# The end of a block unit in the first embedding stage, queued on ScalarE behind the copy between its PSUM banks

## The chip, the core and the metric

The kernel runs on one core of one Trainium2 chip. The metric is the device time of one execution in microseconds (us), as a median over runs. Engine names are those of the profile: PE is TensorE's matmul and PEld its weight load, DVE is VectorE, ACT is ScalarE, POOL is GpSimd, SP is SyncE, which issues most of the DMAs.

## The reference

Two layers of a decoder trunk on 512 tokens with 1024 features, all in float32. Each layer is a mixer (layer 0: windowed attention beside a short convolution; layer 1: chunked gated linear attention), a gated MLP with a causal convolution, and a per-layer embedding; each adds to x.

```python
for i in range(DEPTH):
    h = _rms_norm(x, mix_norm[i])
    x = x + (attn_conv_mixer(h) if i % 2 == 0 else gla_mixer(h))
    x = x + _conv_ffn(_rms_norm(x, ffn_norm[i]), ...)
    x = x + _per_layer_embedding(x, p[i], ple_norm[i], ple_w_gate[i], ple_w_proj[i])

def _per_layer_embedding(x, p_i, norm, w_gate, w_proj):
    gate = jax.nn.sigmoid(_rms_norm(x, norm) @ w_gate)      # 1024 x 1024
    return gate * (p_i @ w_proj)                            # 256 x 1024
```

The change lies in the embedding of layer 0, the function `ple0`. What it leaves behind, x after the embedding, is the input of layer 1's mixer: the gated linear attention, whose first step is again an RMS norm and a projection.

## The kernel before

**Data.** x stays in SBUF as `xT`, eight tiles of 128 features by 512 tokens. A float32 product is made of three matmuls of rounded halves: each operand is split into a rounded high part h and the remainder l, and h·h, h·l and l·h are summed (`mm3`, lines 162 to 164; lines 879 to 881 inside a block product). Such a split costs one ScalarE instruction (the rounding, L109 or L112) and one VectorE instruction (the remainder, L110 or L113). Weights are split the same way when they have been loaded: L142 and L143 in `cut`, L826 and L827 in `cut_blocks`. The high parts go into tiles called `wh`, of which there are three buffers; the low parts go into `wl`.

**The norm.** The scale 1/rms of a token is applied after the product, as the tile `R`. So a stage that changes x ends each feature tile m by writing the rounded product of x and the next norm's gain (`b`, by L112 and L113), by squaring x on ScalarE (L1369 for m = 0, L1372 after it) and by adding the squares into `acc` on VectorE (L1373). When all eight are there, TensorE transposes `acc` (L329), and VectorE sums it (L331).

**The embedding stage of layer 0.** The gate's 1024 output features are made in four units of two tiles (256 features). Units 0 and 1 are plain products (`plain`). Units 2 and 3 are block units: a 2 by 2 block product in seven products instead of eight (`seven`), whose parts run in this order on TensorE, with these copies between PSUM banks on ScalarE:

```python
        product(X[:, left], plain, 1, tokens(1, 0))
        product(Y[:, left], t2, 0, s2)
        self.copied = nc.scalar.copy(X[:, right], Y[:, left])
        yield
        last = self.cut_blocks(od)
        product(X[:, right], t13, 1, s3)
        self.turned_over = nc.scalar.copy(Y[:, right], X[:, right])
        yield
        product(Y[:, left], last, 1, s4)
        product(X[:, right], last, 0, tokens(1, 1))
        yield X, Y, more
```

The first copy shown is L900, the second, `turned_over`, is L904. The product behind L904 writes the bank that L904 writes too, so it waits for it. `seven` is a generator: the loop of `ple0` places other matmuls at its `yield`s.

**The loop.** `ple0` goes over u = 1, 2, 3. Turn u makes the gate's unit u (plain for u = 1, a block unit for u = 2 and 3) and ends the unit before it: it applies the sigmoid to the gate of tiles 2u - 2 and 2u - 1 (L1358), projects p for these two tiles (`proj`, two steps of three matmuls each), and calls `finish` for each. The last unit is ended after the loop. In turn u = 2 or 3 the two projections stand between the parts of the block product; the first tile's projection and the first step of the second come ahead of the product whose end releases L904, and the second's second step, three matmuls, stands between that product and the product that waits for L904. In u = 2 the loop also cuts unit 3's weights, in a context `tc.issue_after(self.turned_over.ins)`.

`finish(m, s, pj)` does six to seven things for one tile: on VectorE the gate times the projection (L1363), x plus that (L1364), the remainder of the rounding (L113) and the sum of squares (L1373); on ScalarE the rounding (L112) and the squares (L1372, or L1369). It issues no DMA and no matmul.

**What sets the order.** Inside this stage TensorE's order is the order of the program (`tc.manual_schedule(engines={ET.PE})`). The other engines' queues are ordered by the framework's planner: it goes through the program in a simulated time and gives each engine the instruction that is ready, the one traced earlier first. `tc.issue_after(ins)` adds, to each instruction that the block traces on the engine of `ins`, an edge of order: it is put behind `ins` on that engine's queue, without a wait for its end. Other engines get no such edge. In layer 1's mixer the planner orders TensorE too.

Of the kernel before, what the change touches and what calls it, by code (L numbers as in the profile page):

```python
# [56 lines left out]
class Kernel:  # L57
# [1235 lines left out]
    def ple0(self, fp):  # L1293

        nc, a, tc = self.nc, self.a, self.tc
        xg, forms = self.xg, []
        wg = a["ple_w_gate"][0].rearrange("(k p) n -> p k n", p=P)
        wp = a["ple_w_proj"][0].rearrange("(k p) n -> p k n", p=P)  # L1300
        units = ND // 2

        def loaded(u):
            raw = self.raw(ND, 2 * P)
            nc.sync.dma_start(raw, wg[:, :, 2 * P * u : 2 * P * (u + 1)])
            return raw

        def sums(j):
            rows = [self.fp.tile([P, S], F32, tag=tag, name=self.nm("sum")) for tag in ("b0", "b0", "b1", "b1")]
            for u in range(2):  # L1310
                m = 2 * j + u
                nc.scalar.activation(rows[u], self.xT[m], AF.Copy, scale=self.g_ple[0][:, m : m + 1])
            forms.append(self.block_sums(rows))

        def square():
            return fp.tile([P, S], F32, tag="z", name=self.nm("z"), bufs=3)

        def sevens(u):

            raw = loaded(u)  # L1320
            ev, od = self.by_parity(raw)
            first = self.first_forms(ev, od, raw)
            yield
            t13 = self.cut_blocks(ev)
            yield self.seven(od, (first, t13, self.more_forms(ev, od)), xg, forms, square)

        def plain(w, c):
            pg = self.ps()
            for k in range(ND):
                self.mm3(pg, w(k, c * P, (c + 1) * P), xg[k], start=k == 0, stop=k == ND - 1)  # L1330
            return pg

        def projection():
            raw = self.raw(2, D)
            nc.sync.dma_start(raw, wp)
            h, l = (self.four(fp).rearrange("p (k c) n -> p k (c n)", k=2) for _ in range(2))
            for k in range(2):
                nc.scalar.activation(h[:, k], raw[:, k], AF.Copy)
                nc.vector.tensor_tensor(l[:, k], raw[:, k], h[:, k].bitcast(F32), ALU.subtract)
            return h, l  # L1340

        def proj(m):

            pj = self.ps()
            c = slice(m * P, (m + 1) * P)
            for k in range(2):
                self.mm3(pj, (wph[:, k, c], wpl[:, k, c]), pT[k], start=k == 0, stop=k == 1)
                yield pj

        def sigmoid(pg, more=None):  # L1350
            s = self.half()
            if more is None:
                nc.vector.tensor_tensor(s, pg, R, ALU.mult)
            else:
                h2 = lambda x: x.rearrange("p (u t) -> p u t", u=2)
                nc.vector.tensor_tensor(h2(s), h2(pg), more.unsqueeze(1).to_broadcast([P, 2, S // 2]), ALU.add)
                nc.vector.tensor_tensor(s, s, R, ALU.mult)
            nc.scalar.activation(s, s, AF.Sigmoid)  # L1358
            return s

        def finish(m, s, pj):
            x = self.xT[m]
            nc.vector.tensor_tensor(s, s, pj, ALU.mult)  # L1363
            nc.vector.tensor_tensor(x, x, s, ALU.add)  # L1364
            hl = self.pair(self.fp, "b0", "b1")
            self.split(hl, x, self.g_mix[1][:, m : m + 1])
            self.xg.append(hl)
            if m == 0:
                nc.scalar.activation(self.acc, x, AF.Square)  # L1369
            else:  # L1370
                sq = square()
                nc.scalar.activation(sq, x, AF.Square)  # L1372
                nc.vector.tensor_tensor(self.acc, self.acc, sq, ALU.add)  # L1373

        src = a["p"][0, 0].rearrange("(t p) e -> p t e", p=P)
        pin = [fp.tile([P, NT, P], F32, tag="z", name=self.nm("pin"), bufs=3) for _ in range(2)]
        for e in range(2):
            nc.sync.dma_start(pin[e], src[:, :, e * P : (e + 1) * P])
        w = self.cut(loaded(0), "b")
        for j in range(ND // 2):  # L1380
            sums(j)
        with tc.manual_schedule(engines={ET.PE}):
            gates = [plain(w, 0)]
            self.end_norm()
            w1 = self.cut(loaded(1), "b")
            gates.append(plain(w, 1))
            R = self.spread()
            pT = self.load_p(0, fp, pin)
            wph, wpl = projection()
            self.begin_norm(("b0", "b1"))  # L1390
            def sigmoids():
                return [sigmoid(*(g if isinstance(g, tuple) else (g,))) for g in gates]

            ready = sevens(2)
            next(ready)
            steps = next(ready)
            for u in range(1, units):
                m = 2 * u - 2
                gates = sigmoids()
                pjs = [proj(m + c) for c in range(2)]  # L1400
                if u == 1:
                    new = []
                    for c in range(2):
                        new.append(plain(w1, c))
                        next(pjs[c])
                        pjs[c] = next(pjs[c])
                else:
                    more = u + 1 < units
                    if more:
                        ready = sevens(u + 1)  # L1410
                        next(ready)
                    next(steps)
                    next(pjs[0])
                    next(steps)
                    pjs[0] = next(pjs[0])
                    next(pjs[1])
                    next(steps)
                    if more:
                        with tc.issue_after(self.turned_over.ins):
                            after = next(ready)  # L1420
                    pjs[1] = next(pjs[1])
                    X, Y, V = next(steps)
                    new = [X, (Y, V)]
                    if more:
                        steps = after
                for c in range(2):
                    finish(m + c, gates[c], pjs[c])
                gates = new
            gates = sigmoids()
            for c in range(2):  # L1430
                pj = proj(ND - 2 + c)
                next(pj)
                finish(ND - 2 + c, gates[c], next(pj))
            self.end_norm()
# [648 lines left out]
```

## Time and profile before

| what | us |
|---|---|
| median of 3 runs (lowest to highest) | 1204.29 (1204.18 to 1205.54) |
| the profiled execution | 1203.8 |
| its span, first to last instruction | 1202.0 |
| PE busy in it | 1194.0 |
| DVE busy | 989.3 |
| ACT busy | 681.1 |
| granted TensorE clock | 1.00 of full speed |

The profile is of one execution. Its times count from the span's start; the embedding stage of layer 0 lies between about 530 and 586 us. A row of a timeline shows the start, the duration, the engine, the line of the kernel, the operation and its tiles, and in brackets the idle time of the engine before it with what ended that. Matmuls are pipelined: the distance between two starts is shorter than the duration of one, and the distance is what counts.

### The profile page before, as it was taken

The numbers are of one execution on the slowest core, as the hardware profiler recorded it, in microseconds if no ns is written. First come the engines' busy times: TensorE is split into PE (matmuls) and PEld (weight loads), VectorE is DVE, ScalarE is ACT, GpSimd is POOL, SyncE is SP. The second block draws the span as 40 slices with busy tenths as digits, with TensorE's granted clock in tenths as the row PEclk, the third lists the DMA queues.
The fourth block names the chain that finished last, engine by engine and source line by source line (L and its number), as shares of the span: only waits on it lengthen the run. The fifth ranks groups of instructions, "written<-read, shape, count | busy, mean of one in ns | idle before, by whom it ended". The sixth has DMA issues, their size and how long they took to land.

```text
span 1202.0 us, 17888 instructions
## 1 busy us (share of the span) xinstructions
PE 1194.0 (99%) x7085; PEld 1037.6 (86%) x7085; DVE 989.3 (82%) x1563; ACT 681.1 (57%) x1109; POOL 43.7 (4%) x64
## 2 busy tenths in 40 slices
PE   9999999999999999999999999999999999999998
PEld 8877788999899889888988988889999999888887
DVE  6786587899999996789769876677999999978595
ACT  7466465656555744566563555565555656645374
POOL 2600000000000000000100000000000000000000
PEclk9999999999999999999999999999999999999999
DMA  7221322323233342232422222313242423322501
GB/s 222 90 88 39 97 79 70 129 83 119 92 104 107 107 139 97 97 106 63 140 66 69 71 71 70 106 54 122 71 140 71 139 72 128 127 88 97 210 1 70
DMA packets 110839, 117.61 MB, mean 98 GB/s; under 512 B 2808, under 2 KB 105778, under 8 KB 110756
## 3 DMA queue, kind: packets, MB, share of 16 engines
q1 hardware_dynamic: 109920, 115.88, 29.7%
q8 instruction: 55, 0.90, 0.3%
q0 software_dynamic: 560, 0.42, 0.3%
q10 hardware_dynamic: 276, 0.18, 0.1%
q14 instruction: 28, 0.23, 0.1%
HBM read 114.37 MB, written 2.10 MB: 97 GB/s over the span
## 4 chain that ended last, share of the span: by engine, by line
PE 89%; DVE 6%; ACT 2%; issue 1%; POOL 1%; DMA 0%; SPq 0%; DVEq 0%; ACTq 0%; POOLq 0%
PE ps L162 11%; PE ps L163 11%; PE ps L164 11%; PE pa L163 7%; PE pa L162 7%; PE pa L164 7%; PE ps L879 6%; PE ps L881 6%; PE ps L880 6%; PE pa L879 2%; PE pa L881 2%; PE pa L880 2%; DVE wl L143 1%; PE ps L1484 1%; PE ps L1483 1%
## 5 line engine op out<-in xcount | busy, mean ns | idle before, releaser
L142 ACT ACTIVATE wh<-raw 128x1024 fp32r<-128x1024 f32 (+4 forms) x146 | 145.8, 999 | 124.5 <-PE ps L163 78.8
L143 DVE TENSOR_TENSOR wl<-raw,wh 128x1024 fp32r<-128x1024 f32 (+4 forms) x146 | 168.1, 1151 | 40.7 <-ACT wh L142 39.9
L826 ACT ACTIVATE wh<-raw 128x1024 fp32r<-128x1024 f32 x84 | 89.2, 1062 | 120.6 <-DVE raw L851 65.1
L939 DVE SCALAR_TENSOR_TENSOR zt<-z,vfa,zt 128x510 f32<-128x510 f32 (+1 forms) x176 | 130.6, 744 | 5.3 <-ACT zt L937 4.7
L827 DVE TENSOR_TENSOR wl<-raw,wh 128x1024 fp32r<-128x1024 f32 x84 | 102.6, 1221 | 21.3 <-ACT wh L826 21.2
L937 ACT ACTIVATE zt<-z,vfb 128x512 f32<-128x512 f32 x88 | 71.0, 810 | 21.5 <-DVE four L990 8.3
L162 PE MATMUL ps<-b,wh 128*128 128x512 f32 x192 | 76.8, 400 | 0.0
L163 PE MATMUL ps<-b,wh 128*128 128x512 f32 x192 | 75.1, 391 | 0.0
L164 PE MATMUL ps<-b,wl 128*128 128x512 f32 x192 | 75.0, 391 | 0.0
L879 PE MATMUL ps<-four,wh 128*128 128x256 f32 x248 | 69.4, 280 | 0.7 <-ACT ps L904 0.7
L163 PE MATMUL pa<-a,wh 128*128 128x512 f32 x176 | 69.0, 392 | 0.0
L163 PE MATMUL pa<-b,wh 128*128 128x512 f32 x176 | 69.0, 392 | 0.0
L162 PE MATMUL pa<-a,wh 128*128 128x512 f32 x176 | 69.0, 392 | 0.0
L162 PE MATMUL pa<-b,wh 128*128 128x512 f32 x176 | 69.0, 392 | 0.0
L881 PE MATMUL ps<-four,wl 128*128 128x256 f32 x248 | 68.8, 277 | 0.0
L880 PE MATMUL ps<-four,wh 128*128 128x256 f32 x248 | 68.6, 277 | 0.0
L164 PE MATMUL pa<-a,wl 128*128 128x512 f32 x176 | 68.4, 389 | 0.0
L164 PE MATMUL pa<-b,wl 128*128 128x512 f32 x176 | 68.4, 389 | 0.0
L162 PE MATMUL ps<-a,wh 128*128 128x512 f32 x128 | 50.6, 395 | 0.0
L162 PE MATMUL ps<-uh,wh 128*128 128x512 f32 x128 | 50.3, 393 | 0.0
L163 PE MATMUL ps<-a,wh 128*128 128x512 f32 x128 | 50.2, 392 | 0.0
L163 PE MATMUL ps<-ul,wh 128*128 128x512 f32 x128 | 50.1, 391 | 0.0
(488 smaller groups left out, 3577.4 us busy)
## 6 DMA issues: line engine op xcount, KB each, us to landing
raw<-in_ffn_w_up_dram SPq DMA_DIRECT2D x44, 1024.0 KB, 5.0
raw<-in_ffn_w_down_dram SPq DMA_DIRECT2D x13, 1024.0 KB, 4.8
raw<-in_hy_w_in_dram SPq DMA_DIRECT2D x8, 1024.0 KB, 5.1
raw<-in_gla_w_in_dram SPq DMA_DIRECT2D x8, 1024.0 KB, 5.2
raw<-in_ffn_w_down_dram SPq DMA_DIRECT2D x8, 768.0 KB, 4.2
raw<-in_ple_w_gate_dram SPq DMA_DIRECT2D x6, 1024.0 KB, 4.8
raw<-in_hy_w_out_dram SPq DMA_DIRECT2D x16, 256.0 KB, 4.0
raw<-in_gla_w_out_dram SPq DMA_DIRECT2D x4, 1024.0 KB, 4.8
```

The lines of the kernel that those rows point to most:

```text
L142: nc.scalar.activation(hv, v, AF.Copy)
L143: nc.vector.tensor_tensor(lv, v, hv.bitcast(F32), ALU.subtract)
L162: mm(out, lh, rh, start=start, stop=False, **kw)
L163: mm(out, lh, rl, start=False, stop=False, **kw)
L164: mm(out, ll, rh, start=False, stop=stop, **kw)
L826: nc.scalar.activation(h, src, AF.Copy)
L827: nc.vector.tensor_tensor(l, src, h.bitcast(F32), ALU.subtract)
L879: mm(out, wh, xh, start=first and j == 0, stop=False, **kw)
L880: mm(out, wh, xl, start=False, stop=False, **kw)
L881: mm(out, wl, xh, start=False, stop=j == ND // 2 - 1, **kw)
L937: nc.scalar.activation(y, z, AF.Identity, scale=w2[:, f : f + 1], bias=bb[:, f : f + 1])
L939: nc.vector.scalar_tensor_tensor(out=y[:, tap:], in0=z[:, : S - tap], scalar=w[:, f : f + 1], in1=y[:, tap:], op0=ALU.mult, op1=ALU.add,)
```

## The change

In the turns u = 2 and u = 3, what `finish` traces on ScalarE for the two tiles of the unit before (L112 and L1372 for tiles 2 and 3, then for tiles 4 and 5) gets an edge of order behind `turned_over`, the copy L904 of the block unit that this turn makes. In the turn u = 1 there is no block unit, and the units ended after the loop are left alone. VectorE's part of `finish` gets no edge.

```diff
--- before.py
+++ after.py
@@ -1423,8 +1423,11 @@
                     new = [X, (Y, V)]
                     if more:
                         steps = after
-                for c in range(2):
-                    finish(m + c, gates[c], pjs[c])
+                with ExitStack() as es:
+                    if u > 1:
+                        es.enter_context(tc.issue_after(self.turned_over.ins))
+                    for c in range(2):
+                        finish(m + c, gates[c], pjs[c])
                 gates = new
             gates = sigmoids()
             for c in range(2):
```

## The prediction

> **What bounds the kernel now.** I read the page first, then the waits of the stage that the change touches, then the timelines of its engines.
>
> ```profile
> span 1202.0 us, 17888 instructions
> PE 1194.0 (99%) x7085; PEld 1037.6 (86%) x7085; DVE 989.3 (82%) x1563; ACT 681.1 (57%) x1109; POOL 43.7 (4%) x64
> ```
>
> TensorE is busy for 1194.0 of 1202.0 us, so there are 8.0 us without a matmul in flight in the whole kernel. Any gain is one of those gaps, or matmuls that stand closer. ScalarE is idle for 43% of the time: its work counts only where TensorE waits for one of its instructions. In the embedding stage there is one such wait (columns: total us, times, longest):
>
> ```profile
> PEld ps L879 <- ACT ps L904: 1.6, 2, 0.8
> PE ps L879 <- ACT ps L904: 0.7, 2, 0.4
> ```
>
> L904 is the copy from bank X to bank Y. There are two such waits, in the turns u = 2 and u = 3 of the loop. ScalarE around the first, and TensorE beside it (start, duration, idle before and its releaser):
>
> ```profile
> 557.34 0.36 ACT L900 COPY ps<-ps 128x256 f32<-128x256 f32 x1 [0.35 <-PE ps L881]
> 559.60 0.72 ACT L112 ACTIVATE b<-xT,vec 128x512 fp32r<-128x512 f32 x1 [1.90 <-DVE xT L1364]
> 560.23 0.61 ACT L1372 ACTIVATE z<-xT 128x512 f32<-128x512 f32 x1
> 560.75 0.36 ACT L904 COPY ps<-ps 128x256 f32<-128x256 f32 x1
> 561.05 1.06 ACT L826 ACTIVATE wh<-raw 128x1024 fp32r<-128x1024 f32 x1
> ```
> ```profile
> 557.02 0.28 PE L881 MATMUL ps<-four,sq 128*128 128x256 f32 x1
> 559.79 0.28 PE L881 MATMUL ps<-four,wl 128*128 128x256 f32 x1
> 560.13 0.40 PE L163 MATMUL ps<-four,four 128*128 128x512 f32 x1
> 560.37 0.39 PE L164 MATMUL ps<-four,four 128*128 128x512 f32 x1
> 561.16 0.38 PE L879 MATMUL ps<-four,wh 128*128 128x256 f32 x1 [0.40 <-ACT ps L904]
> 561.38 0.28 PE L880 MATMUL ps<-four,wh 128*128 128x256 f32 x1
> 561.50 0.28 PE L881 MATMUL ps<-four,wl 128*128 128x256 f32 x1
> ```
>
> The reader should see three things. The product that the copy reads ends at 559.79 + 0.28 = 560.07. ScalarE is then inside L112, the rounding of x's feature tile 2, and runs its squares (L1372) too before the copy at 560.75. And TensorE, after three matmuls of the projection, stands until 561.16. So the copy comes late because of exactly the two instructions that the change moves.
>
> **The change, part by part.** It adds no arithmetic and no DMA, and moves nothing on the DMA, POOL or TensorE queues. It says only that on ScalarE the L112 and the squares of tiles 2 and 3 follow the copy of u = 2, and those of tiles 4 and 5 the copy of u = 3. Tiles 3 and 5 follow it today already; tiles 2 and 4 change places.
>
> *Turn u = 2.* How soon would a free ScalarE start the copy? L900 waited for the same kind of matmul: that began at 557.02, ended at 557.30, and L900 began at 557.34, 0.04 later. So the copy would start at 560.07 + 0.04 = 560.11, not 560.75: 0.64 us earlier. From the start of the copy to the matmul that it releases are 561.16 - 560.75 = 0.41 us, so L879 would start at 560.52. Without any wait it could start at 560.37 + 0.23 (the distance of the two projection matmuls above) = 560.60. But the next one comes 0.22 after a delayed L879, against 0.12 (561.50 - 561.38) in the stream. Then L880 comes at 560.52 + 0.22 = 560.74 at the earliest by the wait and 560.72 by the stream: I take 560.74, against 561.38 today. The gain is 0.64 us; its bounds are 0.40 (the idle time in the row of L879) and 0.66 (no trace of the wait left).
>
> The weight load shows why I don't take the 0.40:
>
> ```profile
> 561.16 0.19 PEld L879 LDWEIGHTS ps<-four,wh 128*128 128x128 f32 x1 [0.84 <-ACT ps L904]
> ```
>
> The load waits with its matmul and starts in the same instant. The Trainium skill (TensorE: Matmul & The Clock Gate, section "Architectural detail: the array is 16× 32×32, not 1× 128×128") says that TensorE can pull a weight load ahead of matmuls in flight; were it so here, the step behind L879 would be the normal one, and the gain 561.16 - 560.60 = 0.56, an estimate by that page, instead of 0.64. This trace does not agree at this place, with 0.84 us of waiting before the load, so the row decides.
>
> *Turn u = 3.* ScalarE and TensorE there:
>
> ```profile
> 570.62 0.37 ACT L900 COPY ps<-ps 128x256 f32<-128x256 f32 x1
> 572.58 0.72 ACT L112 ACTIVATE b<-xT,vec 128x512 fp32r<-128x512 f32 x1 [1.60 <-DVE xT L1364]
> 573.73 0.36 ACT L904 COPY ps<-ps 128x256 f32<-128x256 f32 x1
> 574.03 0.81 ACT L142 ACTIVATE wh<-raw 128x736 fp32r<-128x736 f32 x1
> 577.91 0.81 ACT L142 ACTIVATE wh<-raw 128x736 fp32r<-128x736 f32 x1
> 578.62 0.62 ACT L1358 ACTIVATE zt<-zt 128x512 f32<-128x512 f32 x1
> ```
> ```profile
> 572.77 0.28 PE L880 MATMUL ps<-four,wh 128*128 128x256 f32 x1
> 572.89 0.28 PE L881 MATMUL ps<-four,wl 128*128 128x256 f32 x1
> 574.15 0.38 PE L879 MATMUL ps<-four,wh 128*128 128x256 f32 x1 [0.29 <-ACT ps L904]
> ```
>
> The same sum gives a copy at 572.89 + 0.28 + 0.04 = 573.21 in place of 573.73, a gain of 0.52. But something else can now step in front. L142 behind the copy cuts the next stage's weights. It needs a buffer wh, and the product that the copy waits for is the last reader of one: its last use of wh is L880, one matmul ahead of the L881 that frees the copy. An idle ScalarE therefore has L142 ready 0.12 us before the copy. Nothing holds L142 back: in u = 2 the weight cut is bound behind the copy by the context that the kernel has there already, in u = 3 there is no such line. What the order then becomes, the MLP's down stage shows, where the same product runs with ScalarE idle:
>
> ```profile
> 468.17 1.06 ACT L142 ACTIVATE wh<-raw 128x1024 fp32r<-128x1024 f32 x1 [2.35 <-PE ps L880]
> 469.14 0.36 ACT L904 COPY ps<-ps 128x256 f32<-128x256 f32 x1
> 483.54 1.06 ACT L142 ACTIVATE wh<-raw 128x1024 fp32r<-128x1024 f32 x1 [2.34 <-PE ps L880]
> 484.51 0.36 ACT L904 COPY ps<-ps 128x256 f32<-128x256 f32 x1
> 1085.71 1.06 ACT L142 ACTIVATE wh<-raw 128x1024 fp32r<-128x1024 f32 x1 [2.29 <-PE ps L880]
> 1086.67 0.37 ACT L904 COPY ps<-ps 128x256 f32<-128x256 f32 x1
> ```
>
> Each time ScalarE is idle, L880 releases L142, and the copy follows it. So I expect L142 at 572.77 + 0.28 + 0.04 = 573.09 and the copy 0.71 later (577.91 to 578.62), at 573.80: 0.07 later than today, not 0.52 earlier. Bounds for this turn: -0.52 to +0.07; I take +0.07, since the down stage shows that order each time.
>
> *What waits behind the moved instructions.* On ScalarE, L826 (the weights of unit 3) now comes ahead of L112 for tile 2, since it is traced earlier and is ready. On VectorE, L113 of tile 2 (the low part of the rounding) and the sum of squares follow L112. VectorE is the neighbour to watch:
>
> ```profile
> 560.35 0.75 DVE L113 SCALAR_TENSOR_TENSOR b<-xT,vec,b 128x512 fp32r<-128x512 f32 x1 [0.79 <-ACT b L112]
> 573.34 0.75 DVE L113 SCALAR_TENSOR_TENSOR b<-xT,vec,b 128x512 fp32r<-128x512 f32 x1 [0.79 <-ACT b L112]
> 585.00 0.68 DVE L1373 TENSOR_TENSOR acc<-acc,z 128x512 f32<-128x512 f32 x1
> ```
> ```profile
> 579.74 0.33 PE L162 MATMUL ps<-wh,b 128*128 128x368 f32 x1
> 585.92 0.52 PEld L329 LDWEIGHTS pa<-cf,acc 128*128 128x128 f32 x4
> ```
>
> The rounded tiles are first read at 579.74, about 19 us after tile 2 is made and still 6 us after tile 4, in the order of the features: that cover is ample. The squares are not: their sum ends at 585.68, and TensorE loads it at 585.92, 0.24 us later. If TensorE comes 0.57 us earlier and VectorE does not, L329 would have to come some matmuls later in TensorE's queue. That queue is written out by hand only up to the end of this stage; from 579.74 on the framework's planner orders it, and value matmuls that need no squares are there to stand in front. So I cost this at nothing, and name below what it costs if the cover is gone.
>
> *Sum.* -0.64 + 0.07 = -0.57 us. The profiled execution took 1203.8 us, its span of 1202.0 and 1.8 around it; so 1203.2 by that execution. The median of the runs shown, 1204.29, lies 0.49 above it; the forecast on its scale is 1204.29 - 0.57 = **1203.7 us**. That is 0.05%, and about 0.2% (2.4 us) is what a measurement of this kernel can tell from no change.
>
> **The rivals.** *Both stalls go:* if the planner keeps the copy ahead of L142 in u = 3, the sum is -0.64 - 0.52 = -1.16, or 1203.1 us. For it speaks that only 0.12 us part the two in readiness; against it the down stage.
>
> *The squares take it back, and more* (slower). TensorE meets L329 at the same place in its queue, and VectorE is late. TensorE can then gain no more than 0.24 there, and each microsecond that VectorE slips is paid. VectorE slips if its queue keeps L113 of tile 2 at its place: L112 now follows the copy (560.11, and 0.30 to the next instruction, as 560.75 to 561.05) and L826 (1.06 by its row), so it starts at 561.47, not 559.60; a slip of up to 1.87 us. The result is slower from a slip of 0.24 on, and at most 1.87 - 0.24 = +1.6 us, or 1205.9. Against it: VectorE has L1363 and L827 to do in that time, and the planner may put those first; then the slip is a few tenths, and the time near 1204.4.
>
> *The planner's order in the next stage breaks* (slower). In the gated attention behind this stage TensorE has almost no gap, and VectorE in one part none either:
>
> ```profile
> 597.00:815.00 218.00, 217.74 (x1364) 185.27 (x1363) 165.65 (x336) 119.03 (x221) 5.30 (x6) 1.00 0.25 80
> 625.00:650.00 25.00, 25.00 (x232) 20.52 (x231) 24.67 (x62) 10.21 (x20) 0.00 (x0) 1.00 0.13 31
> L143 DVE TENSOR_TENSOR wl<-raw,wh 128x1024 fp32r<-128x1024 f32 (+4 forms) x146 | 168.1, 1151 | 40.7 <-ACT wh L142 39.9
> ```
>
> TensorE (first busy column) idles 0.26 of 218 us; VectorE (third) is busy for 24.67 of 25. The planner works forward in its own time, so a shift upstream can exchange neighbours there, and an order with 0.26 us of gaps can hardly get better. The price of one VectorE weight cut (1.15 us) put in front of what TensorE waits for is at most 1.15; it decides against the gain from the first one, and beyond 2.4 us from three: 3 x 1.15 - 0.57 = +2.9, or 1207.2. Nothing in the trace says that it happens; only the missing slack speaks for it.
>
> *Faster by over 2.4 us* needs more than the stalls of this stage: the same reshuffle, in a kernel whose gaps are 8.0 us in all. That the edges do nothing is excluded: today L112 at 559.60 and 572.58 stands ahead of the copy that it must follow.
>
> **How the numbers follow.** One stall goes, forecast: 0.38. Both go: 0.13. The squares take it back: 0.19. All three lie within 0.2%, so 0.70 for no visible change. The next stage breaks: 0.20, slower by over 0.2%. A lucky reshuffle: 0.10, faster. The range starts at the edge of the lucky case, 1201.9, which leaves out its 0.10, and ends at the price of three cuts, 1207.2, which leaves out about half of the 0.20.
>
> **What the next profile should show.** In u = 2 the copy L904 follows the last L881 within 0.1 us and L112 of tile 2 comes after it; the wait of TensorE's L879 there is below 0.1. In u = 3 an L142 of 128x736 stands directly ahead of the copy, and L879 waits as today. The first value matmul comes about 0.6 us earlier than 579.74, and L329 has moved a few matmuls back in TensorE's queue without a gap. The forecast is wrong if L142 is behind the copy in u = 3 (then -1.2), if TensorE idles before L329, or if gaps appear between 597 and 815 that are not there now.

## The result, and the profile after

| | us |
|---|---|
| before, same chip | 1204.75 median (1203.98 to 1206.14, 10 runs) |
| after | 1207.89 median (1205.62 to 1208.72, 10 runs) |
| ratio | 1.0024, 95% interval 1.0016 to 1.0033 |
| profiled execution after | 1207.76, span 1206.0 |

Slower by 3.1 us, where 0.6 faster was forecast; the value lies above the range. A second measurement, on the chip of later controls (edge_again, below), gave 1207.01 against 1203.94, ratio 1.0027 [1.0016, 1.0039].

The turn u = 2 first: ScalarE and then TensorE of after (start, duration, idle before and its releaser).

```profile
560.07 0.36 ACT L904 COPY ps<-ps 128x256 f32<-128x256 f32 x1 [2.46 <-PE ps L881]
560.33 1.07 ACT L826 ACTIVATE wh<-raw 128x1024 fp32r<-128x1024 f32 x1
561.29 0.71 ACT L112 ACTIVATE b<-xT,vec 128x512 fp32r<-128x512 f32 x1
```
```profile
560.28 0.39 PE L164 MATMUL ps<-four,four 128*128 128x512 f32 x1
560.50 0.36 PE L879 MATMUL ps<-four,wh 128*128 128x256 f32 x1
560.70 0.28 PE L880 MATMUL ps<-four,wh 128*128 128x256 f32 x1
```

The copy starts at 560.07 instead of 560.75, L826 comes next and L112 behind it, as forecast. TensorE's L879 starts at 560.50 instead of 561.16, 0.66 earlier. Of that, 0.09 us stood ahead of the change already: the projection matmul in front of it, L164, starts at 560.28 here and at 560.37 before. From L164 to L879 it is 0.22 us here and was 0.79, so the copy itself gave 0.57. The gain is there. TensorE's rows in the list of waits of the stage show what came in its place (total us, times, longest):

```profile
PE ps L162 <- DVE zt L1353: 2.1, 1, 2.1
PE ps L879 <- ACT ps L904: 0.4, 1, 0.4
PE ps L162 <- ACT vt L1651: 0.2, 1, 0.2
```

The first row is new, and three times what TensorE lost to the copy before (0.7). It is the first projection matmul of u = 3. The group that it takes its PSUM tile from (`self.ps()`) has four banks; the one due to it still holds the bank X of unit 2's gate, and VectorE's L1353 (the gate times R) is its last reader. Here is VectorE before the change (L113 of tile 2, at 560.35, stands in the prediction), then TensorE there:

```profile
561.02 0.68 DVE L1373 TENSOR_TENSOR acc<-acc,z 128x512 f32<-128x512 f32 x1
561.62 0.68 DVE L1363 TENSOR_TENSOR zt<-zt,ps 128x512 f32<-128x512 f32 x1
562.22 1.22 DVE L827 TENSOR_TENSOR wl<-raw,wh 128x1024 fp32r<-128x1024 f32 x1
563.36 0.68 DVE L1364 TENSOR_TENSOR xT<-xT,zt 128x512 f32<-128x512 f32 x1
563.96 0.68 DVE L858 TENSOR_TENSOR raw<-raw 128x512 f32<-128x512 f32 x1
564.56 0.68 DVE L1353 TENSOR_TENSOR zt<-ps,R 128x512 f32<-128x512 f32 x1
565.16 0.68 DVE L861 TENSOR_TENSOR raw<-raw 128x512 f32<-128x512 f32 x1
```
```profile
565.25 0.28 PE L881 MATMUL pa<-a,wl 128*128 128x256 f32 x1
565.37 0.43 PE L162 MATMUL ps<-four,four 128*128 128x512 f32 x1
```

L1353 ends at 564.56 + 0.68 = 565.24 and the projection starts at 565.37: just in time, with about 0.1 us to spare. There is no idle time to see, so no view of waits names this edge. The same two places after the change:

```profile
560.70 0.69 DVE L1363 TENSOR_TENSOR zt<-zt,ps 128x512 f32<-128x512 f32 x1 [1.23 <-PE ps L164]
561.43 1.23 DVE L827 TENSOR_TENSOR wl<-raw,wh 128x1024 fp32r<-128x1024 f32 x1
562.57 0.75 DVE L113 SCALAR_TENSOR_TENSOR b<-xT,vec,b 128x512 fp32r<-128x512 f32 x1
563.24 0.68 DVE L858 TENSOR_TENSOR raw<-raw 128x512 f32<-128x512 f32 x1
563.84 0.68 DVE L1373 TENSOR_TENSOR acc<-acc,z 128x512 f32<-128x512 f32 x1
564.44 0.68 DVE L861 TENSOR_TENSOR raw<-raw 128x512 f32<-128x512 f32 x1
565.04 0.68 DVE L827 TENSOR_TENSOR sq<-raw,sq 128x512 fp32r<-128x512 f32 x1
565.64 0.68 DVE L1364 TENSOR_TENSOR xT<-xT,zt 128x512 f32<-128x512 f32 x1
566.25 0.68 DVE L1353 TENSOR_TENSOR zt<-ps,R 128x512 f32<-128x512 f32 x1
```
```profile
564.58 0.28 PE L881 MATMUL pa<-a,wl 128*128 128x256 f32 x1
566.98 0.50 PE L162 MATMUL ps<-four,four 128*128 128x512 f32 x1 [2.13 <-DVE zt L1353]
```

L113 and L1373 of tile 2 used to run from 560.35 on. Now L112 is late, VectorE stands idle for 1.23 us until 560.70, and then does both in the middle of its busiest stretch. They stood ahead of L1353 before, too, as did L1364 of tile 3. New ahead of it are L861 and a weight cut (L827 of `sq`), 1.20 us by their distances. The later start of the stretch (560.70 in place of 560.35) adds 0.35, and the step behind L1363 (0.73 in place of 0.60) 0.13: together they make the 1.69 us, but for rounding, by which L1353 moves, from 564.56 to 566.25. Why the planner puts L861 and the cut first now isn't shown. The projection moves from 565.37 to 566.98. TensorE had 0.66 us in hand, so it loses 1.61 + 0.66 = 2.27 there.

Then the clock. Windows of 1 us of after; the first busy column is TensorE, the last but two the granted clock:

```profile
565.00:566.00 1.00, 0.00 (x0) 0.00 (x0) 1.00 (x3) 1.00 (x3) 0.00 (x0) 1.00 0.00 0
566.00:567.00 1.00, 0.02 (x1) 0.02 (x1) 1.00 (x3) 1.00 (x3) 0.00 (x0) 1.00 0.00 0
567.00:568.00 1.00, 1.00 (x3) 0.82 (x4) 1.00 (x2) 1.00 (x3) 0.00 (x0) 0.72 0.00 0
568.00:569.00 1.00, 1.00 (x6) 0.93 (x5) 1.00 (x3) 0.15 (x1) 0.00 (x0) 0.50 0.00 0
569.00:570.00 1.00, 1.00 (x7) 1.00 (x7) 1.00 (x2) 0.00 (x0) 0.00 (x0) 0.50 0.07 16
570.00:571.00 1.00, 1.00 (x7) 1.00 (x7) 0.53 (x1) 0.08 (x1) 0.00 (x0) 0.57 0.00 0
```

Two windows with hardly a matmul, then four with a clock of 0.72, 0.50, 0.50 and 0.57. A 256-column matmul takes 0.41 us there, one every 0.21; otherwise 0.28 and 0.11. From the first step of this projection to its second step it is 573.50 - 566.98 = 6.52 us, before it was 570.24 - 565.37 = 4.87:

```profile
573.50 0.40 PE L162 MATMUL ps<-four,four 128*128 128x512 f32 x1
```
```profile
570.24 0.40 PE L162 MATMUL ps<-four,four 128*128 128x512 f32 x1
```

The fall costs 1.65 us. How TensorE stands against before, at places that both traces have: L879 of u = 2 -0.66; first projection of u = 3 +1.61; its second step +3.26; L879 of u = 3 +3.35 (574.15 to 577.50); the transposes behind the value matmuls (L341) +3.42; the end of the span +4.0. So 2.27 + 1.65 = 3.92 us are lost between 564.6 and 573.5, 0.66 had been gained before, and some 0.7 come behind it. Of these, 0.43 come at the first query of the next stage, which starts 0.79 us behind L341 (600.47) and before the change 0.36 behind it (596.62).

The profile is one execution. Of the ten runs of after, the six with a mean granted clock of 0.998 or 0.999 took 1207.76 to 1208.72; the four with 1.000 took 1205.62, 1205.97, 1206.64 and 1207.71. So the fall probably isn't in every execution. The mean alone doesn't prove one: 0.999 stands in runs of the kernel before as well.

### The profile page after: what moved, and what is told of

Read it like the earlier page. It is cut to its first block, busy times and chain, and to the rows that moved or that the text cites. A ratio compares the mean times of both kernels' runs of the same rounds, so it can differ in the third digit from the quotient of the medians.

```text
span 1206.0 us, 17888 instructions
## 1 busy us (share of the span) xinstructions
PE 1195.8 (99%) x7085; PEld 1039.0 (86%) x7085; DVE 990.2 (82%) x1563; ACT 681.5 (57%) x1109; POOL 43.7 (4%) x64
## 4 chain that ended last, share of the span: by engine, by line
PE 87%; DVE 7%; ACT 2%; issue 1%; POOL 1%; DMA 1%; ACTq 0%; SPq 0%; DVEq 0%; POOLq 0%
PE ps L162 11%; PE ps L163 11%; PE ps L164 11%; PE pa L163 7%; PE pa L162 7%; PE pa L164 7%; PE ps L879 6%; PE ps L881 6%; PE ps L880 6%; PE pa L879 2%; PE pa L881 2%; PE pa L880 2%; DVE wl L143 1%; PE ps L1487 1%; PE ps L1485 1%
## 5 line engine op out<-in xcount | busy, mean ns | idle before, releaser
L142 ACT ACTIVATE wh<-raw 128x1024 fp32r<-128x1024 f32 (+4 forms) x146 | 145.8, 999 | 127.9 <-PE ps L163 78.6
L143 DVE TENSOR_TENSOR wl<-raw,wh 128x1024 fp32r<-128x1024 f32 (+4 forms) x146 | 168.3, 1152 | 42.5 <-ACT wh L142 41.7
L826 ACT ACTIVATE wh<-raw 128x1024 fp32r<-128x1024 f32 x84 | 89.3, 1063 | 120.3 <-DVE raw L851 65.0
L827 DVE TENSOR_TENSOR wl<-raw,wh 128x1024 fp32r<-128x1024 f32 x84 | 102.7, 1222 | 21.1 <-ACT wh L826 21.0
L164 PE MATMUL ps<-b,wl 128*128 128x512 f32 x192 | 75.0, 390 | 0.0
L879 PE MATMUL ps<-four,wh 128*128 128x256 f32 x248 | 69.4, 280 | 0.4 <-ACT ps L904 0.4
L164 PE MATMUL pa<-b,wl 128*128 128x512 f32 x176 | 68.4, 389 | 0.0
L164 PE MATMUL pa<-a,wl 128*128 128x512 f32 x176 | 68.4, 389 | 0.0
```

What stands on the lines that cost most here:

```text
L142: nc.scalar.activation(hv, v, AF.Copy)
L143: nc.vector.tensor_tensor(lv, v, hv.bitcast(F32), ALU.subtract)
L164: mm(out, ll, rh, start=False, stop=stop, **kw)
L826: nc.scalar.activation(h, src, AF.Copy)
L827: nc.vector.tensor_tensor(l, src, h.bitcast(F32), ALU.subtract)
L879: mm(out, wh, xh, start=first and j == 0, stop=False, **kw)
```

## The experiments

Fourteen runs, in four groups. Each group has its own runs of the kernel before, and the medians of these differ between chips (1203.9 to 1204.6), so the column to read is the difference to before of the same group. The ratio is not that of the two medians, and where both are near nothing their signs can differ.

| run | median | before | difference | ratio, 95% interval |
|---|---|---|---|---|
| only_u2 | 1205.7 | 1204.6 | +1.1 | 1.0015 [1.0006, 1.0024] |
| only_u3 | 1204.97 | 1204.6 | +0.4 | 1.0007 [0.9998, 1.0016] |
| proj_other_banks | 1204.52 | 1204.6 | -0.1 | 1.0004 [0.9996, 1.0013] |
| filled_wait | 1207.02 | 1204.6 | +2.4 | 1.0025 [1.0014, 1.0035] |
| two_banks_edge | 1203.23 | 1204.33 | -1.1 | 0.9991 [0.9982, 1.0000] |
| two_banks_no_edge | 1203.74 | 1204.33 | -0.6 | 0.9993 [0.9984, 1.0002] |
| early_gate_read | 1204.06 | 1204.33 | -0.3 | 1.0002 [0.9993, 1.0011] |
| only_u3_cut_behind | 1206.42 | 1204.33 | +2.1 | 1.0018 [1.0009, 1.0027] |
| squares_only | 1207.46 | 1203.92 | +3.5 | 1.0028 [1.0016, 1.0041] |
| early_read_query_bank | 1202.98 | 1203.92 | -0.9 | 0.9993 [0.9984, 1.0001] |
| edge_query_bank | 1205.82 | 1203.92 | +1.9 | 1.0019 [1.0011, 1.0028] |
| query_bank_no_edge | 1203.64 | 1203.94 | -0.3 | 0.9998 [0.9989, 1.0007] |
| early_read_query_bank_2 | 1203.04 | 1203.94 | -0.9 | 0.9994 [0.9985, 1.0002] |
| edge_again | 1207.01 | 1203.94 | +3.1 | 1.0027 [1.0016, 1.0039] |

**One turn at a time: only_u2, only_u3.**

```diff
-                    if u > 1:
+                    if u == 2:      # only_u3: u == 3
```

> The edges in the turn u = 2 alone. Theory A (bank and clock): VectorE's L1353, which empties bank X of unit 2, comes behind L113, L1373 and L1364 in its queue; the first projection of u = 3 needs that bank and waits about 2.1 us, and the granted clock falls behind the wait. All of this is made by u = 2, so this kernel is as slow as the whole change: 2 to 4 us above the kernel before. Theory B (the late rounding and squares of four tiles, or the order of the next stage): half the edges, about half the loss, 1 to 2 us, and no wait of 2 us at the projection.

> The edges in the turn u = 3 alone. Theory A: VectorE's queue up to L1353 of u = 3 is that of the kernel before, so there is no wait for the bank; L142 steps ahead of the copy, so that stall stays. Within 0.6 us of the kernel before, clock 1.00 throughout. Theory B: 1 to 2 us slower.

The edge in u = 2 alone brings the wait for L1353, 2.2 us in its profile, with the clock at 0.57 behind it (568 to 572); that execution took 1208.21. Eight of its eleven runs lie at 1205.36 to 1206.03, seven of them with a mean granted clock of 1.000: probably the wait without a fall of the clock. With the edge in u = 3 alone the wait for L1353 is not there, and the two waits for the copy stay, 0.8 us in sum. So the wait comes with the edge of u = 2, the very turn in which the forecast saw the gain. But the median of only_u2, +1.1, misses the 2 to 4 us that theory A gave it, and +1.1 and +0.4 don't add up to the 3.1 of the whole change. How the rest divides (how often the clock falls, the chip, what stands behind this stage) isn't shown.

**Another bank for the projections: proj_other_banks.** The projections use the other group of four banks; all else is the changed kernel, and VectorE's queue up to L1353 is in the same order.

```diff
-            pj = self.ps()
+            pj = self.pa()
```

> The whole change, with the projections of p in the other four PSUM banks, so that they don't need the bank that L1353 empties. The queues of VectorE and ScalarE in this stage are in the same order as with the change. Theory A: no wait at the projection, clock 1.00, 0.3 to 1.0 us faster than the kernel before (the stall of u = 2 gone, that of u = 3 kept). Theory B: as slow as the change, about 3 us above the kernel before, since nothing on VectorE or ScalarE has changed places.

The wait for L1353 is gone although L1353 runs as late as in after, and the clock stays at 1.00. The loss is gone too, but the gain of 0.3 to 1.0 us that was expected is not seen. The profiled execution shows a place where it can go; it took 1206.35, 1.8 more than the median, so this wait is not that of most runs:

```profile
PE ps L162 <- ACT vt L1651: 1.9, 1, 1.9
```

That is the first query of the next stage. It needs a bank that holds values, which ScalarE empties with L1651; ahead of that on ScalarE stand two cuts of the next stage's weights (L142), which wait for 1 MB that can be requested only when VectorE's last cut of the embedding stage has set its buffer free. ScalarE of this run:

```profile
595.13 1.06 ACT L142 ACTIVATE wh<-raw 128x1024 fp32r<-128x1024 f32 x1 [9.08 <-DMA raw<-in_gla_w_in_dram]
...
597.39 1.06 ACT L142 ACTIVATE wh<-raw 128x1024 fp32r<-128x1024 f32 x1
...
598.50 0.55 ACT L1651 ACTIVATE vt<-ps,rtok 128x352 f32<-128x352 f32 x1
```

Before, the first emptying (L1648, the same line there) runs from 595.86 to 596.41 and the query starts at 596.62: about 0.2 us of slack. So a second chain with hardly any slack stands behind the first, and its length hangs on how fast the 1 MB lands (issues from 580 to 605 us, median us from issue to landing; first proj_other_banks, then after):

```profile
raw<-in_gla_w_in_dram SPq DMA_DIRECT2D x3, 1024.0 KB, 7.3
```
```profile
raw<-in_gla_w_in_dram SPq DMA_DIRECT2D x3, 1024.0 KB, 5.8
```

**The clock by itself: filled_wait.** The changed kernel with nine more matmuls of 512 columns, of ones into a spare bank, ahead of the projection of u = 3, so that TensorE works while it waits.

```diff
                     next(steps)
+                    if u == 3:
+                        spare = self.pa()
+                        rhs = self.ones_r.unsqueeze(1).to_broadcast([P, NT, P])
+                        for _ in range(9):
+                            nc.tensor.matmul(spare, self.ones_r, rhs, start=True, stop=True)
                     next(pjs[0])
```

> The whole change, with nine matmuls of ones (128x512, 0.23 us each, their result unread) ahead of the first projection of u = 3, where TensorE waits. Theory A: the wait for the bank is as long, but TensorE is not idle in it for more than some tenths of a us; the granted clock stays 1.00, and the kernel is 1 to 2 us above the kernel before instead of 3. If the clock has no part in it (the wait alone), it is as slow as the change, 3 us above, or slower.

The projection starts as late as in after (567.17), but the clock stays at 1.00: from its first step to its second it is 4.89 us, as before the change (4.87) and not as in after (6.52). L341 comes at 598.24 against 599.68. The median hardly follows, +2.4, where 1 to 2 was expected. In the profiled execution, 1208.50, the 1 MB took 8.0 us to land, and the query then waited 2.4 us for the value banks. So the clock's part is shown up to L341, and in this execution the second chain took it back; for the other executions that isn't shown.

**Another place in VectorE's queue: early_gate_read.** The banks stay as they are; the products that read the gate's banks get a higher priority, so the planner puts L1353 (L1354 here) ahead of L861 and the sum of squares.

```diff
-                nc.vector.tensor_tensor(s, pg, R, ALU.mult)
+                with tc.high_priority(offset=60):
+                    nc.vector.tensor_tensor(s, pg, R, ALU.mult)
```

> The changed kernel with the products that read X's and Y's banks for the gate given a higher priority, so that VectorE's queue takes the product of unit 2 ahead of the rounding and the sum of squares of the third tile; the banks stay as they were. Theory A (the bank comes free late because of the place in VectorE's queue): the first projection of u=3 waits under 0.3 us, the clock stays at 1.00, and the median lies at 1204.0 to 1205.2, 2.5 to 3.5 below the changed kernel's 1207.9; a wait of 0 to 2.5 us for the value banks may show. Rival (the projections are late for another reason than that queue, such as the number of banks): wait of 2 us and 1207 to 1208 as before.

```profile
562.46 0.75 DVE L113 SCALAR_TENSOR_TENSOR b<-xT,vec,b 128x512 fp32r<-128x512 f32 x1
563.13 0.69 DVE L858 TENSOR_TENSOR raw<-raw 128x512 f32<-128x512 f32 x1
563.73 0.68 DVE L1354 TENSOR_TENSOR zt<-ps,R 128x512 f32<-128x512 f32 x1
```
```profile
564.59 0.40 PE L162 MATMUL ps<-four,four 128*128 128x512 f32 x1
```

The bank is free at 564.41, and the projection starts at 564.59 without idle time, 0.78 before that of the kernel before; 0.20 of this stands ahead of the change, since L164 of u = 2 starts at 560.17 here and at 560.37 there. The median is 0.3 us below the kernel before, where that of the changed kernel is 3.1 above it: the loss is gone with one priority. Two independent repairs, a bank that isn't needed and a bank freed earlier, remove the same loss: the cause in the embedding stage is shown.

**More of the cause: squares_only.** The kernel before with the edge on L1372 of tiles 2 to 5 alone.

```diff
-                nc.scalar.activation(sq, x, AF.Square)
+                with ExitStack() as es:
+                    if m in (2, 3, 4, 5):
+                        es.enter_context(tc.issue_after(self.turned_over.ins))
+                    nc.scalar.activation(sq, x, AF.Square)
```

> The edge on the squares of tiles 2 to 5 alone; the rounding runs as before the change. VectorE's queue then holds two more instructions (the rounding and the sum of squares of the fourth tile, 0.66 and 0.60 us) ahead of the product that frees the bank of unit 2 than in the changed kernel. Theory A (that place in the queue is the loss, and the granted clock falls after a wait of this length): the first projection of u=3 waits 3.0 to 3.7 us, against 2.1, the clock falls to 0.5 to 0.7 for some 3 us behind it, and the median lies 0.5 to 2.0 above the changed kernel's 1207.9: 1208.4 to 1209.9. Rival B (what counts is how much is moved behind the copy, and the squares are the lesser half): 1205 to 1206.5. Rival C (the clock fell in the changed kernel for a reason beside the wait): the clock stays at 1.00 in some run with such a wait.

L113 and L1373 of tile 3 (L1376 here) now stand ahead of L1353 too, 0.66 and 0.61 us by their distances:

```profile
566.26 0.74 DVE L113 SCALAR_TENSOR_TENSOR b<-xT,vec,b 128x512 fp32r<-128x512 f32 x1
566.92 0.68 DVE L1376 TENSOR_TENSOR acc<-acc,z 128x512 f32<-128x512 f32 x1
567.53 0.68 DVE L1353 TENSOR_TENSOR zt<-ps,R 128x512 f32<-128x512 f32 x1
```

The projection comes at 568.26, 1.28 after that of the changed kernel. But 0.59 of this stands ahead of the change: L164 of u = 2 starts at 560.87 here and at 560.28 there. Counted from L164 the projection is 0.69 later, about half of the 1.27 us added. The rest is saved because L113 of tile 2 keeps its place, so that VectorE starts the stretch 0.02 us ahead of L164 (560.85), and in after 0.42 behind it. So the wait grows with what stands ahead of L1353, but it is 2.7 us and not the 3.0 to 3.7 expected. The clock fell, to 0.50 for two windows of 1 us. The median, 1207.46, lies below the 1208.4 to 1209.9 expected; against its own kernel before it is +3.5. From L164 to L879 it is 0.27 us here, 0.79 before the change: to put the squares alone behind the copy removes nearly the whole stall of u = 2.

**The cut ahead of the copy: only_u3_cut_behind.** The edge in u = 3 alone, and the next stage's first weights queued behind the copy too.

```diff
-            v = Values(672, 1040, 352)
+            with tc.issue_after(self.turned_over.ins):
+                v = Values(672, 1040, 352)
```

> The edge for u=3 alone, and the next stage's first weight cuts queued behind the copy between the banks as well. By the prediction's step (the 128x736 cut steps ahead of the copy of u=3 and keeps its wait): here the copy follows the last matmul before it within 0.1 us and the wait of u=3 is under 0.15 us, against 0.4 with the edge alone; the wait of u=2 stays at 0.3 to 0.4. Time within 0.5 us of the run with the edge for u=3 alone (1205.0), since 0.35 us are gained and the value banks' chain, whose cuts come 0.5 to 1 us later on VectorE, can take it back. Rival (the wait of u=3 has another cause than the cut): it stays at 0.3 us or more.

```profile
572.52 0.28 PE L881 MATMUL ps<-four,wl 128*128 128x256 f32 x1
...
573.10 0.39 PE L164 MATMUL ps<-four,four 128*128 128x512 f32 x1
573.33 0.36 PE L879 MATMUL ps<-four,wh 128*128 128x256 f32 x1
```
```profile
572.89 0.36 ACT L904 COPY ps<-ps 128x256 f32<-128x256 f32 x1 [2.23 <-PE ps L881]
```

The copy follows its product by 0.09 us and L879 follows L164 without a gap: the cut was what kept the wait of u = 3 alive. But the time is +2.1, against +0.4 without this second edge, where a difference within 0.5 us was expected. The cuts come later, and TensorE then waits 0.5 us for L1363, 0.4 for the cut L143 and 0.8 for the value banks. Removing 0.4 us of wait cost about 1.7, by runs of two groups.

**The second chain, with and without the edge: two_banks_edge, two_banks_no_edge.** Beside the projections, the first query goes to the other group of banks.

```diff
-            def feature(w, c):
-                ps = self.ps()
+            def feature(w, c, ps=None):
+                ps = self.ps() if ps is None else ps
...
-                    out=o, in0=feature(w, h % 2), ...
+                    out=o, in0=feature(w, h % 2, None if h else self.pa()), ...
```

> The changed kernel with two tile choices altered: the projections of the stage and the first query of the next stage write into the other group of PSUM banks, so neither waits for a bank of the first group. Theory A (the loss is the bank that VectorE's product frees late; what the edge gains is then eaten by a second chain, the landing of the next stage's 1 MB of weights, its cut on ScalarE and the emptying of the value banks behind it): no wait of the first projection or of the first query matmul above 0.3 us, granted clock 1.00 from 560 to 600, and a median of 1203.0 to 1203.9, some 1 us below the 1204.5 of the run with the projections alone in other banks. Rival B (the 1.9 us in that run was one slow transfer, and the value banks bound nothing in most runs): the median stays at 1204.3 to 1204.8. Rival C (the wait only moves on, to the second half of the same weights): a wait of over 1 us inside the first query, median 1204.3 or more.

> The kernel before with the same two tile choices, without the edge. Theory A: the two waits for the copy stay at 0.3 to 0.4 us each, nothing else waits, and the median is 0.5 to 1.1 us above that of the run with the edge and both choices: 1203.9 to 1204.6. Rival B: equal to the kernel before, 1204.6, and to the run with the edge within 0.3. Rival D (the edge itself costs something in the stage that no bank explains): the median is below that of the run with the edge.

With the edge -1.1, where the projections alone gave -0.1, although the 1 MB took 7.8 us in this execution, longer than there. Without the edge -0.6, somewhat below the range expected. No wait of the first query for the value banks is left; with the edge 0.35 us of one for the cut L143 is. In the form with the edge both stalls of the copy are gone, since the planner put three value matmuls in front of L879 of u = 3; without the edge, only the stall of u = 2 is in the list of waits, with 0.4 us.

**Both repairs at their smallest, and what the edge is worth: early_read_query_bank, edge_query_bank, query_bank_no_edge, edge_again.** The first query's bank is changed as above in the first three; early_read_query_bank has the edge and the higher priority as well, edge_query_bank the edge alone. edge_again is the changed kernel.

> The changed kernel with the products that read the gate's banks at a higher priority and the first query of the next stage in a bank of the other group; the projections stay in their banks. Theory A (each of the two repairs takes away one wait): no wait for the bank of unit 2 or for a value bank above 0.3 us, the wait of u=3 for the copy stays at 0.4, and the median is 1203.0 to 1203.9, below the 1204.06 of the early read alone and about the 1203.2 of the run with two groups of banks. Rival (the first query's bank is worth nothing when the transfer is quick): 1204.0 to 1204.4.

> The changed kernel with the first query of the next stage in a bank of the other group, nothing else. Theory A (the changed kernel's loss is the bank of unit 2 and the clock; the value banks cost it 0.2 us at most, since it comes to them late): the wait of 2.1 us for that bank stays, and the median is 1207.0 to 1208.0, within 0.8 us of the changed kernel. Rival (the value banks' chain is the larger part of its loss): 1205 to 1206.

> The kernel before with the first query of the next stage in a bank of the other group, without the edge. Theory A (the value banks take back what a head start upstream gives, and cost the kernel before some tenths of a us in many runs): 0.2 to 0.6 us below the kernel before, and 0.3 to 0.8 above the run with the edge, the early read and the same bank. Rival (all of the 0.9 us that the latter run gained comes from the bank, the edge gives nothing): equal to that run within 0.2 us.

> Taken again beside its control: the changed kernel with the early read and the first query in another bank. Theory A: 0.8 to 1.2 us below the kernel before, 0.3 to 0.8 below the control without the edge. Rival: equal to the control within 0.2 us.

> The changed kernel as it is, on the chip of its controls. Theory A (the loss is the bank of unit 2 and the clock; the value banks add 0.2 to 1 us): 2 to 3.2 us above the kernel before, in two groups, at 1.5 to 2 with the granted clock at 1.000 and at 3 to 4 with a fall. Rival (one level, the clock's fall does not decide): a single group.

early_read_query_bank gave -0.9 twice. Of its waits in the stage only that of u = 3 for the copy is left, 0.4 us.

Its control without the edge and the early read, in the same group, lies 0.60 us higher at the median (1203.64 against 1203.04; in 109 of 121 pairs of runs the kernel with the edge is the faster). The control lacks the early read as well as the edge, and no run has the early read without the edge, so the medians don't divide the 0.60 between the two. The traces show where the time is gained: from L164 to L879 of u = 2 it is 0.23 us with the edge and 0.79 without, and from that L164 to L341 35.37 us in both profiles with the edge, 35.87 in the control: 0.50 less. So a gain close to the forecast's 0.57 exists in this stage, once the two places that take it back are out of the way. Against the kernel before, the intervals of both measurements just include no change, and so does that of two_banks_edge.

edge_query_bank missed its expectation of 1207.0 to 1208.0: 1205.82. Its runs stand in two groups, six at 1205.35 to 1205.82 with a mean granted clock of 0.999 to 1.000, and, but for one at 1206.52, four at 1206.86 to 1207.60, all with 0.998. The wait for L1353 is worth about 1.5 us here and the fall of the clock about 1.7 more in the runs that seem to have it. The changed kernel lost 3.1 in both measurements and this one 1.9. So the value banks may be a larger part of its loss than the 0.2 us of wait in its first profile; the chips differ, and so may the share of runs with a fall, so this isn't shown. The profile of edge_again shows that they can be (waits, then windows):

```profile
PE ps L162 <- DVE zt L1353: 2.2, 1, 2.2
PE ps L162 <- ACT vt L1651: 1.6, 1, 1.6
```
```profile
566.00:568.00 2.00, 1.34 (x8) 1.20 (x9) 2.00 (x5) 1.81 (x4) 0.00 (x0) 1.00 0.00 0
568.00:570.00 2.00, 2.00 (x20) 2.00 (x20) 2.00 (x3) 0.89 (x2) 0.00 (x0) 1.00 0.03 8
```

Here the clock did not fall after the same wait, TensorE reached L341 at 597.75, and then waited 1.6 us for the value banks behind a transfer of 7.3 us; the execution took 1207.02. Fall and slow transfer seem to cover each other in part: whichever is later sets the start of the next stage. The two groups of runs that were expected of edge_again aren't seen: its six runs lie between 1206.04 and 1208.80, and this one, without a fall, is at 3.1 above the kernel before. How much each adds on average isn't settled, nor why the clock falls in one run and not in the next.

## Why the prediction was wrong

1. *Turn u = 2*: right in its mechanism, a little too high in its size. The copy is at 560.07 (forecast 560.11), L112 behind it, and the list has no wait left there. L879 comes 0.66 earlier, forecast 0.64, but that they agree so well is luck: 0.09 of the 0.66 stood ahead of the change, and the copy gave 0.57. The forecast took the longer step behind L879 (0.22 in place of 0.12) for a part of the wait; in after this step is still 0.20, although no wait is listed.
2. *Turn u = 3*: right. L142 stands directly ahead of the copy (576.36, copy 577.08), L879 waits 0.37; TensorE's place moves by +0.09 between that second step of the projection and L879, forecast +0.07. only_u3_cut_behind shows the cause.
3. *What waits behind the moved instructions* ("So I cost this at nothing"): this step failed. It named VectorE as the neighbour to watch and then followed only the data: who reads tile 2's rounding (19 us later) and who reads the squares (0.24 us). It did not follow the queue. L113 and L1373 don't need to be late for their own readers. With them late, VectorE starts its stretch later and takes L861 and a weight cut ahead of L1353, and the bank that L1353 sets free had about 0.1 us to spare. The step was costed at 0; in after it measured +2.27 at the projection of u = 3, and 1.65 more by the clock. proj_other_banks and early_gate_read show the cause; why the planner chose this order stays open.
4. *The rival in which the squares take it back* had the right engine and nearly the size of the slip (L113 up to 1.87 later; it was 562.57 - 560.35 = 2.22), and put the price at the wrong place: L329 moved back some matmuls without a gap, as the forecast itself had said.
5. *The rival of a broken order in the next stage* did not happen: from 597 to 815 TensorE is busy for 217.55 us (before 217.74).
6. The range ended at 1207.2. No case in it had a fall of the clock, since the profile of before shows 1.00 in every slice.

On the clock, the Trainium skill (TensorE: Matmul & The Clock Gate, section "HAM oscillation — how this bites in real kernels") names idle gaps of TensorE above about 3.4 us as what brings the half clock back. This trace agrees on the half (0.50), but not on the gap: 2.13 us were enough here, and 2.16 were not in edge_again. The same page (section "What's actually happening") gives about 3.4 us of sustained work as what brings the full clock back; the low stretch here agrees, if the clock was either 1.00 or 0.50: the four windows then hold 2 x (0.28 + 0.50 + 0.50 + 0.43) = 3.4 us at half, an estimate from their rows. The same sum over windows of 1 us gives 3.4 in the profiles of only_u2, edge_query_bank and squares_only. That section also says that the window of the gate runs freely and isn't started by the kernel, which could let equal gaps end differently; equal gaps did end differently here, and no run shows the window itself.

## What to carry to other kernels

When instructions are moved to a later place, list what changes its place in every queue that they feed, and ask of each instruction that comes later not only who reads its result but which buffer or bank it sets free, and when that is next needed. A handover that is just in time leaves no row in a view of waits: compare the end of the last reader of each bank with the start of its next writer. And before a gain upstream is counted, look for the next chain without slack that must also get shorter; in some profiles here 1 MB of weights set the start of the next stage.

## What the runs showed of the hardware

- A wait of TensorE of 2.1 to 2.7 us was followed by a granted clock of 0.50 for 3.4 us (an estimate from windows of 1 us) in the profiles of after, only_u2, edge_query_bank and squares_only, and not in that of edge_again, which is the kernel of after. Matmuls of 256 columns start every 0.21 us then instead of 0.11. It cost 1.65 us in after. With nine matmuls into a spare bank, put into the wait, the clock stayed at 1.00 in the one profile taken.
- The same requests of 1 MB took a median of 5.2 to 8.0 us from issue to landing in different executions of nearly the same program. The query behind them waited 0.2 us in after, where the two issued from 586 to 600 us took 5.9, and 1.6 us in edge_again, the same kernel, where they took 7.3. That this spreads the times of the other runs isn't shown.
